# A matmul with bias and residual: 1024-row super tiles, and x transposed as fp32 words of two bf16

## The chip, the cores and the metric

The kernel runs on one core of a Trainium2 chip. The metric is the device time of one launch in microseconds (us), lower is better. "Span" is the time from the first to the last instruction in the one profiled execution; a timed run is 1.7 to 1.9 us longer than its span here. The runs compared below are of the same, fast state, with two exceptions that are marked: two experiments had a single look each, which has no state, and one run of the last version was slow.

PE does the matmuls and transposes (PEld in the profile is the loading of its stationary operand, the one held while the columns of the moving operand stream past it). ACT casts, DVE copies and adds, GpSimd (POOL) adds, and SP issues the transfers. SBUF and PSUM are memories on the chip; the results of PE go to PSUM. The "chain" of a profile is the work that ended last, followed back at each step to what released it.

## The reference

```python
batch, m, k, n = 16, 512, 1024, 768        # all float32
def reference(x, weight, bias, residual):
    return (np.matmul(x, weight) + bias + residual).astype(np.float32)
```

x is 33.6 MB, W 3.1 MB, the residual and the output 25.2 MB each: 87 MB to move, and 64 tiles of 128 rows to multiply.

## The kernel before

A super tile is 512 rows, four consecutive rows on each of 128 partitions, so one row of a transfer is 16 KB (x) or 12 KB (residual, output). ACT casts a tile of x to bf16, PE transposes it in eight 128x128 pieces into one PSUM bank, DVE copies it out as `xt`, and PE multiplies it with W in 16 matmuls, two (512 and 256 columns) for each of eight k chunks. GpSimd adds the bias to the residual in SBUF, and DVE adds the PSUM result onto that. For the first eight tiles the residual is not there yet: DVE puts PSUM plus bias into `tmp`, and GpSimd adds `tmp` to the residual later.

```python
J, HEAD, X_BUFS, RO_BUFS = 4, 3, 3, 7
HEAD_ORDER = [("x", 0), ("w", 0), ("x", 1), ("w", 1), ("w", 2), ("x", 2), ("w", 3), ...]
...
    def transp(t):
        pt = ring(ps, "pt", t, 2, [P, n_k, P], BF16)
        for k in range(n_k):                                   # 8 pieces
            nc.tensor.transpose(out=pt[:, k, :], in_=xb[t][:, ts(k, P)], identity=ident)
        xt[t] = ring(sb, "xt", t, 4, [P, n_k, P], BF16)
        nc.vector.tensor_copy(out=xt[t], in_=pt)
    def mm(t, k, n0, nl):
        nc.tensor.matmul(po[t][:, n0:n0 + nl], lhsT=xt[t][:, k, :], rhs=w_sb[:, k, n0:n0 + nl], ...)
...
    for _ in range(WARM_MM): ...            # 11 matmuls on zeros, to warm the clock
    for kind, i in HEAD_ORDER: ...          # three tiles at once, as x and W arrive
...
    for t in range(HEAD, n_t):
        cast(t + 2)
        if (t + 2) % J == J - 1:
            S = (t + 2) // J
            load_x(S + X_BUFS); load_res(S + 2); store(S - 1)
        transp(t + 1)
        ... 16 matmuls of tile t ...
        finish(t - 1)                       # DVE: PSUM + row (or tmp, for t < 8)
        pool_add(...)                       # GpSimd
    ...
    for n0, nl in chunks:                   # last tile: each chunk has its own store
        ... ; finish(n_t - 1, n0, nl); store(S, J - 1, J, n0, nl)
```

(Here and in the edits below, wrappers such as `K_(...)`, which keeps the program order, are left out in places.)

Of the kernel before, what the change touches and what calls it, by code (L numbers as in the profile page):

```python
# [9 lines left out]
FP32 = mybir.dt.float32  # L10
BF16 = mybir.dt.bfloat16
P = 128
J = 4
HEAD = 3
X_BUFS = 3
RO_BUFS = 7
TMP_BUFS = 4
EARLY = 8
WARM_MM = 11
HEAD_ORDER = [  # L20
    ("x", 0), ("w", 0), ("x", 1), ("w", 1), ("w", 2), ("x", 2),
    ("w", 3), ("w", 4), ("w", 5), ("w", 6), ("w", 7),
]


@with_exitstack
def kernel(
    ctx: ExitStack,
    tc: tile.TileContext,
    x: bass.AP,  # L30
    weight: bass.AP,
    bias: bass.AP,
    residual: bass.AP,
    out: bass.AP,
):
    nc = tc.nc
    x2d = x.flatten_outer_dims()
    res2d = residual.flatten_outer_dims()
    out2d = out.flatten_outer_dims()
    M, K = x2d.shape  # L40
    N = weight.shape[1]
    n_k = K // P
    n_t = M // P
    n_s = n_t // J
    chunks = [(0, 512), (512, N - 512)]

    x_d = x2d.rearrange("(S p j) k -> S p j k", p=P, j=J)
    res_d = res2d.rearrange("(S p j) n -> S p j n", p=P, j=J)
    out_d = out2d.rearrange("(S p j) n -> S p j n", p=P, j=J)
    w_d = weight.rearrange("(ko ki) n -> ki ko n", ki=P)  # L50

    const = ctx.enter_context(tc.tile_pool(name="const", bufs=1))
    sb = ctx.enter_context(tc.tile_pool(name="sb", bufs=1))
    ps = ctx.enter_context(tc.tile_pool(name="ps", bufs=1, space=bass.MemoryType.PSUM))

    def ring(pool, name, i, n, shape, dt):
        return pool.tile(shape, dt, name=name, tag=f"{name}{i % n}", bufs=1)

    def psum_o(i):
        return ring(ps, "psum_o", i, HEAD, [P, N], FP32)  # L60

    x_sb, ro, xb, xt, po, tmp = {}, {}, {}, {}, {}, {}
    K_ = tc.keep_in_program_order

    def load_x(S, j0=0, j1=J):
        if S < n_s:
            if j0 == 0:
                x_sb[S] = ring(sb, "x_tile", S, X_BUFS, [P, J, K], FP32)
            K_(nc.sync.dma_start(out=x_sb[S][:, j0:j1, :], in_=x_d[S, :, j0:j1, :]))

    def load_res(S, j0=0, j1=J):
        if S < n_s:
            if j0 == 0:
                ro[S] = ring(sb, "ro", S, RO_BUFS, [P, J, N], FP32)
            K_(nc.sync.dma_start(out=ro[S][:, j0:j1, :], in_=res_d[S, :, j0:j1, :]))

    def store(S, j0=0, j1=J, n0=0, nl=N):
        if 0 <= S < n_s:
            K_(nc.sync.dma_start(
                out=out_d[S, :, j0:j1, n0:n0 + nl], in_=ro[S][:, j0:j1, n0:n0 + nl]  # L80
            ))

    w_st = [
        ring(sb, "ro", RO_BUFS - 2 + h, RO_BUFS, [P, n_k // 2, N], FP32) for h in range(2)
    ]
    w_sb = const.tile([P, n_k, N], BF16, name="w_sb")


    def cast(t):
        if t < n_t:  # L90
            xb[t] = ring(sb, "xb", t, 4, [P, K], BF16)
            K_(nc.scalar.copy(out=xb[t], in_=x_sb[t // J][:, t % J, :]))  # L92

    def transp(t):
        if t < n_t:
            pt = ring(ps, "pt", t, 2, [P, n_k, P], BF16)
            for k in range(n_k):
                K_(nc.tensor.transpose(out=pt[:, k, :], in_=xb[t][:, ts(k, P)], identity=ident))  # L98
            xt[t] = ring(sb, "xt", t, 4, [P, n_k, P], BF16)
            K_(nc.vector.tensor_copy(out=xt[t], in_=pt))  # L100

    def mm(t, k, n0, nl):
        K_(nc.tensor.matmul(  # L103
            po[t][:, n0:n0 + nl], lhsT=xt[t][:, k, :], rhs=w_sb[:, k, n0:n0 + nl],
            start=(k == 0), stop=(k == n_k - 1),
        ))

    def row(t, n0=0, nl=N):
        return ro[t // J][:, t % J, n0:n0 + nl]

    def pool_add(t):
        if t < n_t:
            r = row(t)
            K_(nc.gpsimd.tensor_add(out=r, in0=r, in1=tmp[t] if t < EARLY else bias_sb))  # L114

    def finish(t, n0=0, nl=N):
        if t < 0:
            return
        p = po[t][:, n0:n0 + nl]
        if t < EARLY:  # L120
            tmp[t] = ring(sb, "tmp", t, TMP_BUFS, [P, N], FP32)
            K_(nc.vector.tensor_add(out=tmp[t], in0=p, in1=bias_sb))  # L122
        else:
            K_(nc.vector.tensor_add(out=row(t, n0, nl), in0=p, in1=row(t, n0, nl)))  # L124


    bias_row = const.tile([1, N], FP32, name="bias_row")
    K_(nc.gpsimd.dma_start(out=bias_row, in_=bias[None, :]))  # L128
    warm = const.tile([P, 512], BF16, name="warm")
    K_(nc.vector.memset(warm, 0.0))  # L130
    ones_row = const.tile([1, P], FP32, name="ones_row")
    K_(nc.vector.memset(ones_row, 1.0))
    warm_a = const.tile([1, 2], FP32, name="warm_a")
    K_(nc.vector.memset(warm_a, 0.0))
    K_(nc.scalar.copy(out=warm_a, in_=warm_a))  # L135
    ident = const.tile([P, P], BF16, name="ident")
    make_identity(nc, ident)

    warm_ps = psum_o(0)
    for _ in range(WARM_MM):  # L140
        K_(nc.tensor.matmul(  # L141
            warm_ps[:, 0:512], lhsT=warm[:, 0:P], rhs=warm, start=True, stop=True
        ))
    bias_ps = psum_o(HEAD - 1)
    for n0, nl in chunks:
        K_(nc.tensor.matmul(  # L146
            bias_ps[:, n0:n0 + nl], lhsT=ones_row, rhs=bias_row[:, n0:n0 + nl],
            start=True, stop=True,
        ))
    bias_sb = const.tile([P, N], FP32, name="bias_sb")  # L150
    K_(nc.vector.tensor_copy(out=bias_sb, in_=bias_ps))  # L151


    seen_x, seen_w = [], []
    for kind, i in HEAD_ORDER:
        if kind == "x":
            load_x(0, i, i + 1)
            cast(i)
            transp(i)
            po[i] = psum_o(i)  # L160
            seen_x.append(i)
        else:
            K_(nc.sync.dma_start(out=w_st[i // 4][:, i % 4, :], in_=w_d[:, i, :]))
            K_(nc.vector.tensor_copy(out=w_sb[:, i, :], in_=w_st[i // 4][:, i % 4, :]))  # L164
            seen_w.append(i)
        for t in seen_x if kind == "w" else [i]:
            for k in [i] if kind == "w" else seen_w:
                for n0, nl in chunks:
                    mm(t, k, n0, nl)
    load_x(0, 3, 4)  # L170
    load_x(1, 0, 2)
    load_res(0, 0, 2)
    load_x(1, 2, 4)
    load_res(0, 2, 4)
    load_x(2)
    load_res(1)
    cast(HEAD)
    transp(HEAD)
    cast(HEAD + 1)
    load_x(3)  # L180
    load_res(2)
    for t in range(HEAD - 1):
        finish(t)
        pool_add(t)


    for t in range(HEAD, n_t):
        cast(t + 2)
        if (t + 2) % J == J - 1:
            S = (t + 2) // J  # L190
            load_x(S + X_BUFS)
            load_res(S + 2)
            store(S - 1)
        transp(t + 1)
        po[t] = psum_o(t)
        if t < n_t - 1:
            for k in range(n_k):
                for n0, nl in chunks:
                    mm(t, k, n0, nl)
        finish(t - 1)  # L200
        if t - 1 < EARLY:
            pool_add(t - 1)
        if t + 1 >= EARLY:
            pool_add(t + 1)
    S = n_s - 1
    store(S, 0, J - 2)
    store(S, J - 2, J - 1)
    for n0, nl in chunks:
        for k in range(n_k):
            mm(n_t - 1, k, n0, nl)  # L210
        finish(n_t - 1, n0, nl)
        store(S, J - 1, J, n0, nl)


# [28 lines left out]
```

## Time and profile before

| | before |
|---|---|
| time, median | 216.97 us (216.23 to 218.88) |
| span | 216.1 us |
| PE busy, share of the chain of waits that ended last | 95%, 93% |
| one tile on PE | 3.05 us: 2.60 for 16 matmuls, 0.45 for 8 transposes |
| rate of the transfers, 30 to 190 us | 427 GB/s |
| rate that one tile in 3.05 us asks for | 430 GB/s |

Read it by the last two rows: PE is the engine that the chain follows, but the transfers run at the same pace. The lines themselves stand in the prediction.

### The profile page before, as it was taken

What the parts mean: (1) busy time and instruction counts of PE and PEld (TensorE: products, weight loads), DVE (VectorE), ACT (ScalarE), POOL (GpSimd) and SP (SyncE); (2) the same over time, 40 slices, a digit from 0 to 9 for tenths busy, and PEclk for the clock granted to TensorE, in tenths of its full rate; (3) what the DMA queues carried; (4) which work ended last, traced back from release to release, by engine and by line L of the source; (5) the groups of instructions that cost most, each with busy time, mean ns of one, the idle gap of its engine ahead of it and who ended that gap; (6) DMA issues with size and microseconds to landing.
All of it is one profiled execution on the core that took longest, in us unless ns stands there. A gap on an engine that the chain in (4) does not pass through costs nothing.

```text
span 216.1 us, 3672 instructions
## 1 busy us (share of the span) xinstructions
PE 205.2 (95%) x1551; PEld 132.4 (61%) x1551; DVE 105.1 (49%) x141; ACT 68.0 (31%) x66; POOL 115.3 (53%) x71
## 2 busy tenths in 40 slices
PE   7678799999999999999999999999999999999992
PEld 2335566666666666666666666666666666666651
DVE  0245365445554455445544555445544555445542
ACT  2314416323332333323332333323332333231000
POOL 2000096669928467390928457290936629099600
PEclk9658999999999999999999999999999999999999
DMA  6999999999999999999999999999999999999654
GB/s 179 393 413 418 441 413 429 428 425 431 428 422 431 425 427 421 434 422 421 440 418 436 426 432 420 431 428 422 434 417 438 421 432 424 434 414 416 260 233 176
DMA packets 9265, 87.28 MB, mean 404 GB/s; under 512 B 1056, under 2 KB 1184, under 8 KB 3360
## 3 DMA queue, kind: packets, MB, share of 16 engines
q1 hardware_dynamic: 9216, 87.04, 96.0%
q8 instruction: 12, 0.20, 0.4%
q14 instruction: 5, 0.04, 0.0%
q0 software_dynamic: 32, 0.00, 0.0%
HBM read 61.87 MB, written 25.17 MB: 403 GB/s over the span
## 4 chain that ended last, share of the span: by engine, by line
PE 93%; DVE 3%; DMA 3%; issue 1%; DVEq 0%; POOLq 0%
PE psum_o L103 78%; PE pt L98 13%; DMA bias_row<-in_bias_dram 3%; PE psum_o L146 1%; DVE xt L100 1%; DVE ro L124 1%; DVE tmp L122 0%; DVE bias_sb L151 0%; DVE w_sb L164 0%; DVEq L124 0%; DVEq L100 0%; POOLq L227 0%; POOLq masks.py:199 0%
## 5 line engine op out<-in xcount | busy, mean ns | idle before, releaser
L103 PE MATMUL psum_o<-w_sb,xt 128*128 128x256 bf16 (+1 forms) x1024 | 178.8, 328 | 4.9 <-DVE xt L100 1.6
L103 PEld LDWEIGHTS <-xt 128*128 128x128 bf16 x1024 | 97.8, 98 | 64.9 <-issue 2.2
L114 POOL TENSOR_TENSOR ro<-ro,bias_sb 128x768 f32<-128x768 f32 x56 | 99.7, 1812 | 59.5 <-DMA ro<-in_residual_dram 59.5
L92 ACT CAST xb<-x_tile 128x1024 bf16<-128x1024 f32 x64 | 66.5, 1046 | 127.0 <-PE pt L98 102.8
L100 DVE COPY xt<-pt 128x1024 bf16<-128x1024 bf16 x64 | 44.3, 692 | 94.6 <-PE pt L98 94.6
L124 DVE TENSOR_TENSOR ro<-psum_o,ro 128x768 f32<-128x768 f32 (+2 forms) x57 | 53.3, 935 | 4.9 <-PE psum_o L103 3.0
L98 PEld LDWEIGHTS <-xb 128*128 128x128 bf16 x512 | 34.9, 100 | 9.1 <-ACT xb L92 0.7
L98 PE MATMUL pt<-ident,xb 128*128 128x128 bf16 x512 | 40.1, 223 | 0.0
L114 POOL TENSOR_TENSOR ro<-ro,tmp 128x768 f32<-128x768 f32 x8 | 14.4, 1811 | 27.7 <-DVE tmp L122 26.3
L122 DVE TENSOR_TENSOR tmp<-psum_o,bias_sb 128x768 f32<-128x768 f32 x8 | 7.5, 948 | 0.0
L141 PE MATMUL psum_o<-warm 128*128 128x512 bf16 x11 | 3.9, 531 | 1.2 <-DVE warm L130 1.2
L151 DVE COPY bias_sb<-psum_o 128x768 f32<-128x768 f32 x1 | 1.0, 958 | 8.0 <-PE psum_o L146 8.0
L164 DVE CAST w_sb<-ro 128x768 bf16<-128x768 f32 x8 | 4.0, 553 | 0.0
L146 PE MATMUL psum_o<-bias_row,ones_row 1*128 1x512 f32 (+1 forms) x4 | 2.3, 720 | 1.7 <-DMA bias_row<-in_bias_dram 1.7
L141 PEld LDWEIGHTS <-warm 128*128 128x128 bf16 x11 | 1.3, 129 | 3.3 <-issue 1.9
L146 PEld LDWEIGHTS psum_o<-bias_row,ones_row 1*128 1x128 f32 x4 | 0.9, 234 | 3.0 <-issue 3.0
L135 ACT ACT_TABLE_LOAD x1 | 1.3, 1283 | 0.7 <-PEq L227 0.7
L128 POOL DMA_DIRECT2D bias_row<-in_bias_dram x1 | 0.6, 646 | 0.8 <-POOLq L227 0.8
L130 DVE MEMSET warm<- 128x256 uint32 x1 | 0.3, 272 | 0.9 <-PEq L227 0.9
masks.py:199 POOL TENSOR_SCALAR_AFFINE_SELECT ident<-ident 128x128 bf16<-128x128 bf16 x1 | 0.3, 292 | 0.1
L227 POOL MEMSET const-float32-0.0<- 128x1 f32 x1 | 0.1, 98 | 0.2 <-issue 0.2
masks.py:197 POOL MEMSET ident<- 128x128 bf16 x1 | 0.2, 224 | 0.0
(6 smaller groups left out, 0.7 us busy)
## 6 DMA issues: line engine op xcount, KB each, us to landing
x_tile<-in_x_dram SPq DMA_DIRECT2D x14, 2048.0 KB, 24.5
ro<-in_residual_dram SPq DMA_DIRECT2D x15, 1536.0 KB, 27.8
out_dram<-ro SPq DMA_DIRECT2D x15, 1536.0 KB, 25.3
ro<-in_weight_dram SPq DMA_DIRECT2D x8, 384.0 KB, 8.5
x_tile<-in_x_dram SPq DMA_DIRECT2D x4, 512.0 KB, 7.2
x_tile<-in_x_dram SPq DMA_DIRECT2D x2, 1024.0 KB, 11.2
ro<-in_residual_dram SPq DMA_DIRECT2D x2, 768.0 KB, 11.7
out_dram<-ro SPq DMA_DIRECT2D x1, 768.0 KB, 3.3
```

The lines of the kernel that those rows point to most:

```text
L92: K_(nc.scalar.copy(out=xb[t], in_=x_sb[t // J][:, t % J, :]))
L98: K_(nc.tensor.transpose(out=pt[:, k, :], in_=xb[t][:, ts(k, P)], identity=ident))
L100: K_(nc.vector.tensor_copy(out=xt[t], in_=pt))
L103: K_(nc.tensor.matmul(po[t][:, n0:n0 + nl], lhsT=xt[t][:, k, :], rhs=w_sb[:, k, n0:n0 + nl], start=(k == 0), stop=(k == n_k - 1),))
L114: K_(nc.gpsimd.tensor_add(out=r, in0=r, in1=tmp[t] if t < EARLY else bias_sb))
L122: K_(nc.vector.tensor_add(out=tmp[t], in0=p, in1=bias_sb))
L124: K_(nc.vector.tensor_add(out=row(t, n0, nl), in0=p, in1=row(t, n0, nl)))
L135: K_(nc.scalar.copy(out=warm_a, in_=warm_a))
L141: K_(nc.tensor.matmul(warm_ps[:, 0:512], lhsT=warm[:, 0:P], rhs=warm, start=True, stop=True))
L146: K_(nc.tensor.matmul(bias_ps[:, n0:n0 + nl], lhsT=ones_row, rhs=bias_row[:, n0:n0 + nl], start=True, stop=True,))
L151: K_(nc.vector.tensor_copy(out=bias_sb, in_=bias_ps))
L164: K_(nc.vector.tensor_copy(out=w_sb[:, i, :], in_=w_st[i // 4][:, i % 4, :]))
```

## The change

The intent: fewer and longer transfers (rows of 32 and 24 KB), and half as many transposes. A pair of neighbouring bf16 values of x is taken as one fp32 word; four fp32 transposes move what eight bf16 ones did. After that the two values of a pair lie beside each other in `xt`, so the stationary operand of a matmul is read with a step of two, and W is loaded so that rows 2p and 2p+1 lie on one partition. The start is different too: W is loaded first, the start on three tiles at once and the warming matmuls are gone, and the last store is one piece.

```diff
-J = 4
+J = 8
+X_SLOTS = 2
+RO_SLOTS = 4
...
-    w_d = weight.rearrange("(ko ki) n -> ki ko n", ki=P)
+    w_d = weight.rearrange("(q p e) n -> p q e n", p=P, e=2)
...
-            for k in range(n_k):
-                K_(nc.tensor.transpose(out=pt[:, k, :], in_=xb[t][:, ts(k, P)], identity=ident))
+            words = XB[t % 3].bitcast(FP32)
+            for q in range(n_q):
+                K_(nc.tensor.transpose(out=pt[:, q, :], in_=words[:, ts(q, P)], identity=ident))
...
-            po[t][:, n0:n0 + nl], lhsT=xt[t][:, k, :], rhs=w_sb[:, k, n0:n0 + nl],
+            PO[t % PS][:, n0:n0 + nl], lhsT=XT[t % 3][:, q, :, e],
+            rhs=w_sb[:, q, e, n0:n0 + nl],
...
+    load_w(0); load_w(1); load_x(0, 0, 2); load_w(2); load_w(3)
+    load_x(0, 2, 4); load_x(0, 4, 8)
+    load_res(0); load_x(1); load_res(1)
...
-        store(S, J - 1, J, n0, nl)
+    store(S, 7, 8)
```

(The last block of loads is written on fewer lines here.)

More of the change, by code (lines that the diff above doesn't have):

```diff
@@ L12 @@
 P = 128
-J = 4
-HEAD = 3
-X_BUFS = 3
-RO_BUFS = 7
-TMP_BUFS = 4
-EARLY = 8
-WARM_MM = 11
-HEAD_ORDER = [
-    ("x", 0), ("w", 0), ("x", 1), ("w", 1), ("w", 2), ("x", 2),
-    ("w", 3), ("w", 4), ("w", 5), ("w", 6), ("w", 7),
-]
+J = 8
+X_SLOTS = 2
+RO_SLOTS = 4
+EARLY = 8
+PS = 3
 @with_exitstack
@@ L41 @@
     N = weight.shape[1]
-    n_k = K // P
+    n_q = K // (2 * P)
     n_t = M // P
@@ L49 @@
     out_d = out2d.rearrange("(S p j) n -> S p j n", p=P, j=J)
-    w_d = weight.rearrange("(ko ki) n -> ki ko n", ki=P)
-    const = ctx.enter_context(tc.tile_pool(name="const", bufs=1))
+    w_d = weight.rearrange("(q p e) n -> p q e n", p=P, e=2)
     sb = ctx.enter_context(tc.tile_pool(name="sb", bufs=1))
     ps = ctx.enter_context(tc.tile_pool(name="ps", bufs=1, space=bass.MemoryType.PSUM))
-    def ring(pool, name, i, n, shape, dt):
-        return pool.tile(shape, dt, name=name, tag=f"{name}{i % n}", bufs=1)
@@ L59, in psum_o, with fixed @@
-    def psum_o(i):
-        return ring(ps, "psum_o", i, HEAD, [P, N], FP32)
-    x_sb, ro, xb, xt, po, tmp = {}, {}, {}, {}, {}, {}
+    def fixed(pool, name, n, shape, dt):
+        return [pool.tile(shape, dt, name=f"{name}", tag=f"{name}{i}", bufs=1) for i in range(n)]
+    X = fixed(sb, "x_tile", X_SLOTS, [P, J, K], FP32)
+    R = fixed(sb, "ro", RO_SLOTS, [P, J, N], FP32)
+    XB = fixed(sb, "xb", 3, [P, K], BF16)
+    XT = fixed(sb, "xt", 3, [P, n_q, P, 2], BF16)
+    PO = fixed(ps, "psum_o", PS, [P, N], FP32)
@@ L63 @@
+    PT = fixed(ps, "pt", 2, [P, n_q, P], FP32)
+    (w_sb,) = fixed(sb, "w_sb", 1, [P, n_q, 2, N], BF16)
+    (bias_sb,) = fixed(sb, "bias_sb", 1, [P, N], FP32)
+    (bias_row,) = fixed(sb, "bias_row", 1, [1, N], FP32)
+    (ones_row,) = fixed(sb, "ones_row", 1, [1, P], FP32)
+    (ident,) = fixed(sb, "ident", 1, [P, P], FP32)
+    (warm_a,) = fixed(sb, "warm_a", 1, [1, 2], FP32)
     K_ = tc.keep_in_program_order
+    w_st, tmp = R[2], R[3]
     def load_x(S, j0=0, j1=J):
         if S < n_s:
-            if j0 == 0:
-                x_sb[S] = ring(sb, "x_tile", S, X_BUFS, [P, J, K], FP32)
@@ L69, in load_x @@
-            K_(nc.sync.dma_start(out=x_sb[S][:, j0:j1, :], in_=x_d[S, :, j0:j1, :]))
+            K_(nc.sync.dma_start(out=X[S % X_SLOTS][:, j0:j1, :], in_=x_d[S, :, j0:j1, :]))
     def load_res(S, j0=0, j1=J):
         if S < n_s:
-            if j0 == 0:
-                ro[S] = ring(sb, "ro", S, RO_BUFS, [P, J, N], FP32)
-            K_(nc.sync.dma_start(out=ro[S][:, j0:j1, :], in_=res_d[S, :, j0:j1, :]))
+            K_(nc.sync.dma_start(out=R[S % RO_SLOTS][:, j0:j1, :], in_=res_d[S, :, j0:j1, :]))
@@ L77, in store, with load_w @@
+    def load_w(q):
+        K_(nc.sync.dma_start(out=w_st[:, 2 * q:2 * q + 2, :], in_=w_d[:, q, :, :]))
+        for e in range(2):
+            K_(nc.vector.tensor_copy(out=w_sb[:, q, e, :], in_=w_st[:, 2 * q + e, :]))
     def store(S, j0=0, j1=J, n0=0, nl=N):
@@ L79, in store, with mm @@
             K_(nc.sync.dma_start(
-                out=out_d[S, :, j0:j1, n0:n0 + nl], in_=ro[S][:, j0:j1, n0:n0 + nl]
-            ))
-    w_st = [
-        ring(sb, "ro", RO_BUFS - 2 + h, RO_BUFS, [P, n_k // 2, N], FP32) for h in range(2)
-    ]
-    w_sb = const.tile([P, n_k, N], BF16, name="w_sb")
+                out=out_d[S, :, j0:j1, n0:n0 + nl],
+                in_=R[S % RO_SLOTS][:, j0:j1, n0:n0 + nl],
+            ))
     def cast(t):
         if t < n_t:
-            xb[t] = ring(sb, "xb", t, 4, [P, K], BF16)
-            K_(nc.scalar.copy(out=xb[t], in_=x_sb[t // J][:, t % J, :]))
+            K_(nc.scalar.copy(out=XB[t % 3], in_=X[t // J % X_SLOTS][:, t % J, :]))
     def transp(t):
         if t < n_t:
-            pt = ring(ps, "pt", t, 2, [P, n_k, P], BF16)
-            for k in range(n_k):
-                K_(nc.tensor.transpose(out=pt[:, k, :], in_=xb[t][:, ts(k, P)], identity=ident))
-            xt[t] = ring(sb, "xt", t, 4, [P, n_k, P], BF16)
-            K_(nc.vector.tensor_copy(out=xt[t], in_=pt))
-    def mm(t, k, n0, nl):
+            words = XB[t % 3].bitcast(FP32)
+            pt = PT[t % 2]
+            for q in range(n_q):
+                K_(nc.tensor.transpose(out=pt[:, q, :], in_=words[:, ts(q, P)], identity=ident))
+            K_(nc.vector.tensor_copy(
+                out=XT[t % 3].rearrange("p q m e -> p (q m e)"),
+                in_=pt.rearrange("p q m -> p (q m)").bitcast(BF16),
+            ))
+    def mm(t, n0, nl, q, e):
         K_(nc.tensor.matmul(
-            po[t][:, n0:n0 + nl], lhsT=xt[t][:, k, :], rhs=w_sb[:, k, n0:n0 + nl],
-            start=(k == 0), stop=(k == n_k - 1),
+            PO[t % PS][:, n0:n0 + nl], lhsT=XT[t % 3][:, q, :, e],
+            rhs=w_sb[:, q, e, n0:n0 + nl],
+            start=(q == 0 and e == 0), stop=(q == n_q - 1 and e == 1),
         ))
     def row(t, n0=0, nl=N):
-        return ro[t // J][:, t % J, n0:n0 + nl]
+        return R[t // J % RO_SLOTS][:, t % J, n0:n0 + nl]
     def pool_add(t):
@@ L113, in pool_add @@
             r = row(t)
-            K_(nc.gpsimd.tensor_add(out=r, in0=r, in1=tmp[t] if t < EARLY else bias_sb))
+            K_(nc.gpsimd.tensor_add(out=r, in0=r, in1=tmp[:, t, :] if t < EARLY else bias_sb))
     def finish(t, n0=0, nl=N):
-        if t < 0:
-            return
-        p = po[t][:, n0:n0 + nl]
+        p = PO[t % PS][:, n0:n0 + nl]
         if t < EARLY:
-            tmp[t] = ring(sb, "tmp", t, TMP_BUFS, [P, N], FP32)
-            K_(nc.vector.tensor_add(out=tmp[t], in0=p, in1=bias_sb))
+            K_(nc.vector.tensor_add(out=tmp[:, t, :], in0=p, in1=bias_sb))
         else:
             K_(nc.vector.tensor_add(out=row(t, n0, nl), in0=p, in1=row(t, n0, nl)))
-    bias_row = const.tile([1, N], FP32, name="bias_row")
-    K_(nc.gpsimd.dma_start(out=bias_row, in_=bias[None, :]))
-    warm = const.tile([P, 512], BF16, name="warm")
-    K_(nc.vector.memset(warm, 0.0))
-    ones_row = const.tile([1, P], FP32, name="ones_row")
     K_(nc.vector.memset(ones_row, 1.0))
-    warm_a = const.tile([1, 2], FP32, name="warm_a")
     K_(nc.vector.memset(warm_a, 0.0))
     K_(nc.scalar.copy(out=warm_a, in_=warm_a))
-    ident = const.tile([P, P], BF16, name="ident")
-    make_identity(nc, ident)
-    warm_ps = psum_o(0)
-    for _ in range(WARM_MM):
-        K_(nc.tensor.matmul(
-            warm_ps[:, 0:512], lhsT=warm[:, 0:P], rhs=warm, start=True, stop=True
-        ))
-    bias_ps = psum_o(HEAD - 1)
+    load_w(0)
+    load_w(1)
+    load_x(0, 0, 2)
+    load_w(2)
+    load_w(3)
+    load_x(0, 2, 4)
+    load_x(0, 4, 8)
+    load_res(0)
+    load_x(1)
+    load_res(1)
+    K_(nc.gpsimd.dma_start(out=bias_row, in_=bias[None, :]))
+    make_identity(nc, ident)
+    bias_ps = PO[PS - 1]
     for n0, nl in chunks:
@@ L149 @@
         ))
-    bias_sb = const.tile([P, N], FP32, name="bias_sb")
     K_(nc.vector.tensor_copy(out=bias_sb, in_=bias_ps))
-    seen_x, seen_w = [], []
-    for kind, i in HEAD_ORDER:
-        if kind == "x":
-            load_x(0, i, i + 1)
-            cast(i)
-            transp(i)
-            po[i] = psum_o(i)
-            seen_x.append(i)
-        else:
-            K_(nc.sync.dma_start(out=w_st[i // 4][:, i % 4, :], in_=w_d[:, i, :]))
-            K_(nc.vector.tensor_copy(out=w_sb[:, i, :], in_=w_st[i // 4][:, i % 4, :]))
-            seen_w.append(i)
-        for t in seen_x if kind == "w" else [i]:
-            for k in [i] if kind == "w" else seen_w:
-                for n0, nl in chunks:
-                    mm(t, k, n0, nl)
-    load_x(0, 3, 4)
-    load_x(1, 0, 2)
-    load_res(0, 0, 2)
-    load_x(1, 2, 4)
-    load_res(0, 2, 4)
-    load_x(2)
-    load_res(1)
-    cast(HEAD)
-    transp(HEAD)
-    cast(HEAD + 1)
-    load_x(3)
-    load_res(2)
-    for t in range(HEAD - 1):
-        finish(t)
-        pool_add(t)
-    for t in range(HEAD, n_t):
+    cast(0)
+    cast(1)
+    transp(0)
+    for t in range(n_t):
         cast(t + 2)
@@ L190 @@
             S = (t + 2) // J
-            load_x(S + X_BUFS)
-            load_res(S + 2)
-            store(S - 1)
+            if S + 2 < n_s - 1:
+                store(S - 1)
+                load_x(S + 2)
+                load_res(S + 2)
+            elif S + 2 == n_s - 1:
+                load_x(S + 2, 0, 4)
+                load_x(S + 2, 4, 8)
+                store(S - 1)
+                load_res(S + 2)
+            else:
+                store(S - 1)
         transp(t + 1)
-        po[t] = psum_o(t)
         if t < n_t - 1:
-            for k in range(n_k):
-                for n0, nl in chunks:
-                    mm(t, k, n0, nl)
-        finish(t - 1)
-        if t - 1 < EARLY:
-            pool_add(t - 1)
+            for q in range(n_q):
+                for e in range(2):
+                    for n0, nl in chunks:
+                        mm(t, n0, nl, q, e)
+        if t > 0:
+            finish(t - 1)
+            if t - 1 < EARLY:
+                pool_add(t - 1)
         if t + 1 >= EARLY:
@@ L205 @@
     S = n_s - 1
-    store(S, 0, J - 2)
-    store(S, J - 2, J - 1)
+    store(S, 0, 4)
+    store(S, 4, 6)
+    store(S, 6, 7)
     for n0, nl in chunks:
-        for k in range(n_k):
-            mm(n_t - 1, k, n0, nl)
+        for q in range(n_q):
+            for e in range(2):
+                mm(n_t - 1, n0, nl, q, e)
         finish(n_t - 1, n0, nl)
-        store(S, J - 1, J, n0, nl)
+    store(S, 7, 8)
 _INS = ['x', 'weight', 'bias', 'residual']
```

## The prediction

> **What bounds the kernel now.** I read the page's first two parts, then the chain, the timeline of two tiles in the middle, the groups, and last the windows of the head and the tail.
>
> ```profile
> PE 205.2 (95%) x1551; PEld 132.4 (61%) x1551; DVE 105.1 (49%) x141; ACT 68.0 (31%) x66; POOL 115.3 (53%) x71
> ...
> PEclk9658999999999999999999999999999999999999
> DMA  6999999999999999999999999999999999999654
> GB/s 179 393 413 418 441 413 429 428 425 431 428 422 431 425 427 421 434 422 421 440 418 436 426 432 420 431 428 422 434 417 438 421 432 424 434 414 416 260 233 176
> ...
> PE 93%; DVE 3%; DMA 3%; issue 1%; DVEq 0%; POOLq 0%
> ```
>
> Two things are full at once. PE carries 93% of the chain, and the DMA row is 9 tenths from the second slice to the thirty-seventh. So PE is followed back as the cause of the end, but the transfers have almost no slack. The timeline shows the PE's step (columns: start, length in us, engine, line, operation):
>
> ```profile
> 99.58 0.61 PE L98 MATMUL pt<-ident,xb 128*128 128x128 bf16 x8
> ...
> 102.62 0.61 PE L98 MATMUL pt<-ident,xb 128*128 128x128 bf16 x8
> ...
> 105.67 0.61 PE L98 MATMUL pt<-ident,xb 128*128 128x128 bf16 x8
> ```
>
> One 128-row tile takes 105.67 - 102.62 = 3.05 us with no gap. The chain in order of time splits it into 2.60 us for 16 matmuls and 0.45 us for 8 transposes (56 ns each). In 3.05 us a tile needs 4 + 3 + 3 KB for each of 128 rows, 1.311 MB, which is 430 GB/s. Between 30 and 190 us the queues moved 427 GB/s on average. The two limits are thus within 1% of each other, and a PE that needs less can gain only what the transfers lose at the two ends. Those are in the windows (stretch: length, busy time of PE, PEld, DVE, ACT, POOL, then clock, DMA share, GB/s):
>
> ```profile
> 0.00:2.00 2.00, 0.81 (x2) 0.28 (x3) 0.41 (x3) 1.26 (x1) 0.96 (x6) 1.00 0.08 18
> 2.00:4.00 2.00, 2.00 (x6) 0.76 (x5) 0.00 (x0) 0.21 (x2) 0.40 (x2) 1.00 0.96 243
> 4.00:6.00 2.00, 1.14 (x5) 0.29 (x3) 0.00 (x0) 0.34 (x1) 0.00 (x0) 1.00 0.92 327
> ...
> 200.00:202.00 2.00, 2.00 (x19) 1.43 (x18) 1.23 (x2) 0.00 (x0) 2.00 (x3) 1.00 0.49 209
> 202.00:204.00 2.00, 2.00 (x20) 1.39 (x18) 0.51 (x2) 0.00 (x0) 1.61 (x1) 1.00 0.56 211
> ...
> 206.00:208.00 2.00, 2.00 (x20) 1.37 (x18) 1.14 (x2) 0.00 (x0) 0.00 (x0) 1.00 0.44 184
> 208.00:210.00 2.00, 2.00 (x14) 1.13 (x12) 0.89 (x2) 0.00 (x0) 0.00 (x0) 1.00 0.42 172
> ```
>
> All 87.28 MB at 427 GB/s are 204.4 us; the span is 216.1. The missing 11.7 us are, by adding up (427 - rate)/427 over two-microsecond windows, some 3.5 us at the head (small first rows, empty queue) and some 8 us after 198 us, where the last stores wait for the PE, one tile at a time. That 8 us, plus what the head can give, is all there is to win.
>
> **What the Trainium skill says.** "DMA: Bandwidth & Descriptors", § Bandwidth, measures 425 GB/s for a 16 MB transfer under a fabric ceiling of 435; this trace's 427 agrees, so I count on no faster rate from longer rows than about 1%. "TensorE: Matmul & The Clock Gate", § Terms, says transpose mode is "4× faster for FP32"; § Back-to-back issue gap gives N/2.4 + 2.5 ns, 56 ns for N = 128, which the 56 ns of the bf16 transposes confirm. No fp32 transpose runs in this trace. What does run is the fp32 bias matmul:
>
> ```profile
> L146 PE MATMUL psum_o<-bias_row,ones_row 1*128 1x512 f32 (+1 forms) x4 | 2.3, 720 | 1.7 <-DMA bias_row<-in_bias_dram 1.7
> L98 PE MATMUL pt<-ident,xb 128*128 128x128 bf16 x512 | 40.1, 223 | 0.0
> L98 PEld LDWEIGHTS <-xb 128*128 128x128 bf16 x512 | 34.9, 100 | 9.1 <-ACT xb L92 0.7
> ```
>
> Two instructions leave four records: two passes each. Some 2.3 us for 768 columns, at a mean clock of about 0.7, are 4 to 5 cycles a column. A quarter of four is one cycle a column, if the skill's factor holds. The same page, § Weight-path perf modes, says that the fast weight load is not used for fp32, and allows a column step up to 1,024 elements; § LDWEIGHTS gives P/1.2, 107 ns for 128 columns. So the stride of two in the new matmul's stationary operand should cost nothing, while an fp32 transpose may be paced by its weight load.
>
> **The change part by part.**
>
> 1. *Transposes.* Removed: 8 x 56 ns = 0.45 us a tile. Added: 4 fp32 ones. At one cycle a column 4 x 56 = 0.22 us; paced by a 107 ns load (or two cycles a column) 4 x 107 = 0.43 us; with four cycles 4 x 216 = 0.86 us. The tile period p becomes 2.82, 3.03 or 3.46 us. The PSUM copy still moves 1024 bf16 from one bank, 692 ns from the group of line 100, off the path. Casts (1.05 us), adds on DVE (0.95) and GpSimd (1.81) are unchanged and all under p.
>
> 2. *Head.* W now lands first, in four 6 KB-row loads, with two of the x tiles between. Before the first output tile the queue carries 3.15 MB of W and 1.05 MB of x: 9.8 us at 427 GB/s from about 2 us. DVE has all 8 W casts (553 ns each), the bias copy (0.96) and then the first x copy (0.69) in its program order, so the first matmul is at about 14.7 us, on a cold clock (about 1.8 us lost), as the 11 warming matmuls are gone. The kernel before runs pieces of tiles 0 to 2 from 11.4 us, but is only done with three tiles at about 26; here three tiles are done by 14.7 + 1.8 + 3p = 25 to 26. No gain on the PE. On the DMA side the rows of 6 to 8 KB in place of 3 to 4 KB should fill the first 10 us better: perhaps 1 us of the 3.5.
>
> 3. *First hand-over.* x of super tile 1 is queued behind W, x 0 and residual 0: 14.7 MB, so it lands at 2.5 + 34.4 = 36.9 us. Its first cast and transpose stand in the PE's order before the matmuls of tile 7. PE reaches them at 14.7 + 1.8 + 7 x 2.82 = 36.2 (p = 2.82) or 37.7 (p = 3.03). A stall of 1 to 3 us: the matmuls of tile 7 start at about 39.0 either way. Before they started at 39.25.
>
> 4. *Middle.* A super tile is 10.49 MB, 24.6 us at 427 GB/s, against 8p = 22.6 us or 24.2 us. Two x slots suffice: slot S is released by the cast of tile 8S+7, when PE begins tile 8S+3, nine tiles ahead of its next use. The store of a super tile needs its last tile, but when the queue is behind, that is about 6 us after x lands, inside the 7.4 us of the residual load that follows. So the queue stays full, and with p = 2.82 the kernel runs at the pace of the transfers.
>
> 5. *Tail.* After the last x there remain one residual and four stores, some 15.7 MB or 37 us; PE needs about 9p = 25 us plus some 3 us for the wait on the last residual. So for p = 2.82 the PE is done before the queue, and the store of the last row (1.7 to 2.3 us to land before) is nearly all that lies bare.
>
> Sum if transfers bound it: about 2.5 us until the queue is at full rate, 204.0 us for the data at 427 GB/s, 1.5 us of tail: 208. Sum if PE bounds it: 39.0 + 56p for the start of the last tile, + 2.6 for it, + about 2.2 for its last addition and store. With p = 3.03 that is 213.5; with 2.95, 209; with 3.46, 237.5.
>
> **The rivals.**
>
> - *The fp32 transposes save nothing* (p about 3.03, paced by weight loads): 212 to 215 us. For it: the skill's remark on fp32 weight loads, and fp32 loads that record 234 ns here, against 100 for bf16. Against it: some of each load should lie under the matmul before.
> - *Four cycles a column, or a weight load that no longer runs ahead* (p = 3.2 to 3.5): 223 to 240 us, the PE stays at the centre of the chain and the DMA row falls. For it: the bias matmul's 4 to 5 cycles. Against it: the skill's sentence on transpose mode.
> - *A dry queue*: longer transfers with only two x slots. If a store waits longer than I worked out, each of the 8 super tiles loses one or two microseconds: 212 to 222 us at any p. Against it: step 4.
> - *Longer rows raise the rate* to 432 GB/s, near the ceiling: 205.5 us.
>
> **Range and chances.** I choose the bound by transfers as most likely, weigh in the PE-bound case at 3.0 us, and put the point at 209. That is 3.6% under 216.73; the limit for "faster" is 212.4. About half of the weight lies at 206 to 210, a quarter at 210 to 215, the rest mostly above. Range 205.5 to 217. Faster 0.68, same 0.20, slower 0.12.
>
> **What would show it.** Right: fp32 transposes of about 56 ns in the chain's pieces (0.22 us for four), gaps on PE ended by the cast waiting for x, the chain shifting to DMA, a DMA row at 9 until the last slice, over 420 GB/s in the last 15 us. Wrong: a tile period at or above 3.05 us without gaps, matmul steps longer than 2.60 us a tile (the strided weights then cost something), a DMA row with holes in the middle, or SP waits on stores that coincide with such holes.

## The result

219.57 us (219.35 to 219.74), against 216.97 for the kernel before: ratio 1.010, 95% interval 1.005 to 1.015, so slower by about 1%. A ratio is the mean time of one kernel's fast runs over that of the other's of the same rounds, so it is not quite the ratio of the medians. The prediction was 209.0 with a range of 205.5 to 217.0; the result lies above it.

The page of the changed kernel, first its busy times, slices and chain:

```profile
PE 199.5 (92%) x1259; PEld 130.3 (60%) x1284; DVE 105.0 (48%) x140; ACT 67.8 (31%) x66; POOL 115.3 (53%) x71
...
DMA  6999999999999999999999999999999999995553
GB/s 245 425 434 451 454 394 425 433 471 418 385 392 430 445 418 433 431 434 419 427 431 447 439 410 428 433 451 413 436 413 421 431 433 433 409 397 236 238 211 131
...
PE 79%; DMA 18%; issue 1%; DVE 1%; ACT 0%; ACTq 0%; DVEq 0%
```

The DMA row was to stay at 9 to the end; it falls to 5, 5, 5 and 3 in the last four slices; before it fell to 6, 5 and 4 in the last three. The transfers do not set the end: PE still does. The timeline says why (two tiles, columns as in the prediction):

```profile
97.88 0.60 PE L96 MATMUL pt<-ident,xb 128*128 128x128 f32 x4
98.31 2.76 PE L103 MATMUL psum_o<-w_sb,xt 128*128 128x512 bf16 x16
...
100.91 0.60 PE L96 MATMUL pt<-ident,xb 128*128 128x128 f32 x4
```

and the chain, which counts each group only up to the start of the next:

```profile
98.04 0.44 PE pt L96 x4
98.48 2.60 PE psum_o L103 x16
```

Four fp32 transposes take from 97.88 to the first matmul at 98.31, and the next tile begins at 100.91: the tile period is 3.03 us here and 3.037 on average from tile 7 to tile 62, 2.60 for the matmuls and 0.44 for the transposes. One fp32 transpose costs 110 ns where a bf16 one cost 56. Half as many at twice the price: the period is 0.01 us shorter than before (3.046 on average), 0.6 us over 55 periods.

The groups have the same two terms (count | busy, mean ns of one | idle before):

```profile
L96 PE MATMUL pt<-ident,xb 128*128 128x128 f32 x256 | 39.2, 278 | 2.7 <-ACT xb L89 2.7
L96 PEld LDWEIGHTS pt<-ident,xb 128*128 128x128 f32 x256 | 30.4, 143 | 11.2 <-issue 2.1
```

256 records for 256 instructions, so one pass each, and 39.2 us busy in all where the 512 bf16 ones had 40.1.

Where the kernel became slower is seen in the chain in order of time (start, length, what; short pieces are left out at the dots):

```profile
0.74 4.43 DMA ro<-in_weight_dram
5.18 33.74 DMA x_tile<-in_x_dram
...
39.02 1.05 ACT xb L89
...
40.12 0.66 PE pt L96 x4
40.78 0.05 issue
40.83 2.55 PE psum_o L103 x15
```

The x of super tile 1 landed at 38.92 us, 33.7 us after its issue, and its first cast began at 39.02. PE had nothing from 38.79 to 40.12. The matmuls of tile 7 start at 40.83, in the kernel before at 39.25. And the end, in the timelines: here

```profile
212.98 1.03 PE L103 MATMUL psum_o<-w_sb,xt 128*128 128x256 bf16 x8 [0.85 <-DVE ro L122]
...
214.05 0.43 DVE L122 TENSOR_TENSOR ro<-psum_o,ro 128x256 f32<-128x256 f32 x1 [1.12 <-PE psum_o L103]
```

and in the kernel before

```profile
213.07 0.42 DVE L124 TENSOR_TENSOR ro<-psum_o,ro 128x256 f32<-128x256 f32 x1 [1.12 <-PE psum_o L103]
```

From the end of the last addition to the end of the span are 218.0 - 214.48 = 3.5 us against 216.1 - 213.49 = 2.6 us. In the windows of the tail (columns as in the prediction)

```profile
200.00:205.00 5.00, 4.95 (x34) 3.40 (x34) 2.04 (x4) 0.00 (x0) 0.53 (x1) 1.00 0.20 82
205.00:210.00 5.00, 4.95 (x33) 3.19 (x33) 2.91 (x4) 0.00 (x0) 0.00 (x0) 1.00 0.58 241
```

PE is busy throughout and the transfers are nearly idle, 82 GB/s for five microseconds: the stores wait for tiles, as before, in larger pieces.

So the difference of the spans, 1.9 us, is put together from +1.6 at tile 7, -0.6 from 55 slightly shorter periods and +0.9 in the tail. (The medians of the timed runs differ by 2.6 us. The other 0.7 us are mostly scatter of the kernel before: the spans of its eleven runs that were timed with the first experiments go from 214.4 to 217.2 us, and the profiled one, 216.1, lies about 0.9 above what its median time corresponds to. What makes one run of it shorter than another is open.)

### The profile page after: what moved, and what is told of

The parts are those of the page before. It is cut to its first block, busy times and chain, and to the rows that moved or that the text cites. A ratio compares the mean times of both kernels' runs of the same rounds, so it can differ in the third digit from the quotient of the medians.

```text
span 218.0 us, 3057 instructions
## 1 busy us (share of the span) xinstructions
PE 199.5 (92%) x1259; PEld 130.3 (60%) x1284; DVE 105.0 (48%) x140; ACT 67.8 (31%) x66; POOL 115.3 (53%) x71
## 4 chain that ended last, share of the span: by engine, by line
PE 79%; DMA 18%; issue 1%; DVE 1%; ACT 0%; ACTq 0%; DVEq 0%
PE psum_o L103 68%; DMA x_tile<-in_x_dram 15%; PE pt L96 11%; DMA ro<-in_weight_dram 2%; DVE ro L122 1%; ACT xb L89 0%; ACTq L89 0%; DVEq L122 0%
## 5 line engine op out<-in xcount | busy, mean ns | idle before, releaser
L103 PE MATMUL psum_o<-w_sb,xt 128*128 128x256 bf16 (+1 forms) x999 | 175.3, 327 | 5.3 <-DVE xt L97 3.1
L103 PEld LDWEIGHTS <-xt 128*128 128x128 bf16 x1024 | 100.7, 98 | 64.7 <-DVE xt L97 3.5
L96 PE MATMUL pt<-ident,xb 128*128 128x128 f32 x256 | 39.2, 278 | 2.7 <-ACT xb L89 2.7
L96 PEld LDWEIGHTS pt<-ident,xb 128*128 128x128 f32 x256 | 30.4, 143 | 11.2 <-issue 2.1
L115 POOL TENSOR_TENSOR ro<-ro 128x768 f32<-128x768 f32 x8 | 14.3, 1810 | 29.3 <-DMA ro<-in_residual_dram 25.7
L142 PE MATMUL psum_o<-bias_row,ones_row 1*128 1x512 f32 (+1 forms) x4 | 2.9, 876 | 6.5 <-DMA bias_row<-in_bias_dram 6.5
L120 DVE TENSOR_TENSOR ro<-psum_o,bias_sb 128x768 f32<-128x768 f32 x8 | 7.6, 947 | 0.0
```

The source lines that it names most:

```text
L96: K_(nc.tensor.transpose(out=pt[:, q, :], in_=words[:, ts(q, P)], identity=ident))
L103: K_(nc.tensor.matmul(PO[t % PS][:, n0:n0 + nl], lhsT=XT[t % 3][:, q, :, e], rhs=w_sb[:, q, e, n0:n0 + nl], start=(q == 0 and e == 0), sto ...
L115: K_(nc.gpsimd.tensor_add(out=r, in0=r, in1=tmp[:, t, :] if t < EARLY else bias_sb))
L120: K_(nc.vector.tensor_add(out=tmp[:, t, :], in0=p, in1=bias_sb))
L142: K_(nc.tensor.matmul(bias_ps[:, n0:n0 + nl], lhsT=ones_row, rhs=bias_row[:, n0:n0 + nl], start=True, stop=True,))
```

## The experiments

My theory after reading the traces: the fp32 transpose's price is the failed step, the rest of the prediction would have held with a cheaper one, and the loss against the kernel before lies at tile 7 and in the last store.

### Eight bf16 transposes in the new kernel

```diff
-            words = XB[t % 3].bitcast(FP32)
-            for q in range(n_q):
-                transpose(out=pt[:, q, :], in_=words[:, ts(q, P)], identity=ident)
+            cols = XB[t % 3].rearrange("m (q p e) -> m q e p", p=P, e=2)
+            for q in range(n_q):
+                for e in range(2):
+                    transpose(out=pt[:, q, e, :], in_=cols[:, q, e, :], identity=ident)
```

(`pt`, `xt` and the identity are bf16, and the stationary operand is `XT[t % 3][:, q, e, :]`, without a step.)

> The changed kernel with eight bf16 transposes a tile in place of four fp32 ones, and nothing else undone. Theory A (an fp32 transpose costs 110 ns, so four cost what eight bf16 ones do): the tile period goes from 3.036 to about 3.046 us, the time rises by some 0.6 us, ratio to the changed kernel's 219.57 within 0.5%: about 220. Rival B (the fp32 transposes carry a hidden cost, for instance a switch between fp32 and bf16 weights or the stride of two in the stationary operand, and are why the new kernel is slower): the time falls to 217 or below.

220.21 us (219.91 to 220.33), correct, 0.6 us above the 219.57 (each was timed in its own session; against the kernel before they are 1.012 and 1.010, with intervals that overlap). The transposes now start 3.04 us apart (94.90 and 97.94 in the timeline). Theory A holds, B falls: fp32 words neither help by more than 0.3% nor hurt, and the step of two in the stationary operand costs nothing, as the 16 matmuls take 2.60 us with and without it.

### One transpose of four

```diff
-            for q in range(n_q):
-                transpose(out=pt[:, q, :], in_=words[:, ts(q, P)], identity=ident)
+            transpose(out=pt[:, 0, :], in_=words[:, ts(0, P)], identity=ident)
```

(The copy takes that quarter only, and `xt` is set to zero once at the start.)

> Wrong result on purpose: the changed kernel with one fp32 transpose and a quarter of the copy per tile. It stands for a kernel whose transposes are cheap; all transfers stay. Theory A (my prediction failed only on the size of the transposes, its pace of the transfers was right): tile period about 2.71 us where PE has data, PE waits for x, the DMA row is 9 tenths to the end, and the time is 208 to 211 us. Rival C (two slots of 1024 rows leave the queue dry, so that the transfers would have bound it at a later time anyway): 214 us or more, with holes in the DMA row.

211.04 us (210.75 to 211.23), relative error 0.87, at the upper edge of theory A. Its output is wrong, which doesn't matter for the time. Its page:

```profile
PE   0529999499999999999999995999959999999981
...
DMA  6999999999999999999999999999999999999994
GB/s 234 420 438 454 432 429 431 411 459 407 442 381 434 415 434 426 437 426 464 400 428 428 447 414 448 395 442 454 428 431 412 418 434 428 443 440 404 435 400 176
...
PE 60%; DMA 35%; ACT 2%; issue 1%; DVE 1%; ACTq 0%; DVEq 0%
```

Now the DMA row stays full to the last slice, the holes are on PE, and the chain has 35% of DMA in it. This is the picture that the prediction had drawn for the changed kernel, 2 us above its number. (The run takes 0.11 us of transposes a tile, less than the predicted 0.22, and also copies less; at 0.22 the period would be 2.82 us, still under the 3.07 us that the transfers of a tile take at 427 GB/s.) The tile period is 2.71 us where PE has data (93.16 to 95.87 and to 98.58 in the timeline). So two slots of 1024 rows do not starve the queue, and rival C falls.

### What sets the 110 ns: 96 columns streamed, or 96 loaded

```diff
-                transpose(out=pt[:, q, :], in_=words[:, ts(q, P)], identity=ident)
+                transpose(out=pt[:, q, 0:96], in_=words[0:96, ts(q, P)], identity=ident[0:96, 0:96])
```

> Wrong result on purpose: each fp32 transpose takes 96 rows of x, so 96 columns stream past a weight load of 128 columns. If the streaming sets the 110 ns[...], a transpose takes 82 ns, four take 0.33 us and the tile period is 2.93 us. If the weight load sets it, it stays at 110 ns and 3.036 us.

and the mirror of it

```diff
-                transpose(out=pt[:, q, :], in_=words[:, ts(q, P)], identity=ident)
+                transpose(out=pt[0:96, q, :], in_=words[:, q * P:q * P + 96], identity=ident)
```

> Wrong result on purpose, the mirror of the run before: the fp32 transposes load 96 columns as weights and stream 128. If the weight load sets the 110 ns, a transpose takes 82 ns and the tile period is 2.93 us. If the streaming sets it, it stays at 110 ns and 3.036 us.

The two that ran (one look each, state unknown, wrong on purpose, relative error 0.50) gave 213.92 and 219.62 us. Two transposes' starts in the timeline of the first

```profile
95.89 0.49 PE L96 MATMUL pt<-ident,xb 96*128 96x96 f32 x4
...
98.82 0.49 PE L96 MATMUL pt<-ident,xb 96*128 96x96 f32 x4
```

and of the second

```profile
94.70 0.60 PE L96 MATMUL pt<-ident,xb 128*96 128x128 f32 x4
...
97.74 0.60 PE L96 MATMUL pt<-ident,xb 128*96 128x128 f32 x4
```

With 96 columns streamed the period is 2.93 us and the chain gives 0.33 us for four transposes, 82 ns each; with 96 columns loaded it stays at 3.04 and 0.44. The stream sets the price, not the weight load. 110 ns for 128 columns and 82 for 96 are 0.86 and 0.85 ns a column, twice the 0.44 of the bf16 transposes (56 ns for 128). If those 0.44 are one cycle, as the prediction reads them, this is two. Two things are not told apart: with a square identity the run with 96 columns also has only 96 rows, and what in the stream takes the second cycle is not shown. The width of the fp32 result alone is not it: the matmuls write fp32 to PSUM too, and their 6144 columns of a tile take 2.60 us, 0.42 ns each.

### The wait at tile 7 and the last store, one by one and together

First the order of two loads:

```diff
-    load_res(0)
     load_x(1)
+    load_res(0)
     load_res(1)
```

> The changed kernel with x of super tile 1 queued ahead of residual 0. Theory: of the 2.6 us by which the changed kernel is behind, 1.6 to 1.8 us are the wait at tile 7 for x of super tile 1, which landed at 39.02 us. Queued one 3.15 MB load earlier it lands at about 31.7, PE does not wait, the matmuls of tile 7 start at 39.1 and not at 40.83, and everything after moves by that: 217.8. Rival: the transfers behind it (residual 0 and 1) come later and the wait only moves to the adds: 219.5.

223.38 us (222.99 to 223.47), correct, 3.8 us slower than the changed kernel. The theory fell, and the rival was too mild. PE does not wait at tile 7 any more (its matmuls start at about 39.6), but the timeline shows where it waits instead:

```profile
38.89 12.45 POOL L115 TENSOR_TENSOR ro<-ro 128x768 f32<-128x768 f32 x7 [36.41 <-DMA ro<-in_residual_dram]
...
51.29 1.81 POOL L115 TENSOR_TENSOR ro<-ro,bias_sb 128x768 f32<-128x768 f32 x1
...
53.14 0.96 DVE L122 TENSOR_TENSOR ro<-psum_o,ro 128x768 f32<-128x768 f32 x1 [6.56 <-POOL ro L115]
...
54.75 4.46 PE L103 MATMUL psum_o<-w_sb,xt 128*128 128x512 bf16 x16 [2.83 <-DVE xt L97]
```

The residual of super tile 0 now lands at 38.9 us. Its seven additions stand in GpSimd's order ahead of the first bias addition of super tile 1, which so ends at 53.1 us. DVE waits 6.6 us for it, the PSUM slot is not freed, and PE stops; its 16 matmuls after that take 4.5 us in place of 2.8, and the page gives that slice a clock of 7 tenths. In the changed kernel GpSimd had begun at 28.14 us. An engine that is busy 53% of the time had a deadline all the same.

Then the last store, in two pieces again:

```diff
         finish(n_t - 1, n0, nl)
-    store(S, 7, 8)
+        store(S, 7, 8, n0, nl)
```

> The changed kernel with its last store in two pieces, each after its own addition, as the kernel before has it. Theory: from the last addition's end to the end of the span there are 3.5 us here against 2.6 in the kernel before, because the last store carries all 768 columns of the last tile: the time falls by about 0.9 us, to 218.7. Rival: the store's time is nearly all fixed latency and the queue is still busy with the store before it: 219.5.

219.05 us (218.79 to 219.24), correct: 0.5 us less, between the two guesses. In the trace the span ends 2.9 us after the last addition, against 3.5 without the edit. (The run and the 219.57 are of different sessions, and their ratios to the kernel before do not differ clearly; the pair that follows is of one session.)

And both edits in one kernel:

```diff
-    load_res(0); load_x(1); load_res(1)
+    load_x(1); load_res(0); load_res(1)
...
-    store(S, 7, 8)
+        store(S, 7, 8, n0, nl)
```

> Both edits of the two runs before together. Theory (head wait and tail are the whole loss, and add up): 219.6 - 1.8 - 0.9 = 216.9, the kernel before within 0.5%. If one of the two hides the other: 217.8 or more.

222.83 us (222.26 to 223.62), correct, 0.55 less than the order of loads alone, in the same session. The store's half microsecond adds up; the head's theory is refuted again, for the reason just shown.

If both deadlines are real, a piece of x must come first, but only a piece:

```diff
+    load_x(1, 0, 4)
     load_res(0)
-    load_x(1)
+    load_x(1, 4, 8)
     load_res(1)
```

> The changed kernel with the split last store, and x of super tile 1 in two halves, the first ahead of residual 0 and the second behind it. Theory (two deadlines in one queue: PE needs the first rows of x of super tile 1 by 38 us, GpSimd needs residual 0 by about 34 us or its chain of seven adds, 1.81 us each, makes the first add of super tile 1 late): x lands at about 27 us, residual 0 at about 34, GpSimd is through with its early adds at 47, residual 1 lands at 47, and neither PE nor DVE waits: the matmuls of tile 7 start at 39.1, the time is 217.3, equal to the kernel before within 0.5%. If residual 0 is still too late by 5 us: 221 or more.

217.57 us (217.20 to 218.38), correct, ratio to the kernel before 1.002 (0.997 to 1.008), 0.3 us from the expected 217.3. In its chain in order of time the matmuls follow one another at the same step through tile 7, which starts at 39.28:

```profile
36.24 2.60 PE psum_o L103 x16
39.28 2.60 PE psum_o L103 x16
42.31 2.60 PE psum_o L103 x16
```

The half moved ahead is worth 219.05 - 217.57 = 1.5 us, the split store 0.5. Together they account for 2.0 of the 2.6 us; the rest is within the interval. The kernel before had both: it splits the last store, and it loads half of x of its (smaller) super tile 1, half of residual 0, and then the other halves. The change had dropped that order of loads, which the cut diff above does not show.

### A version that beats both

First try: the older start on three tiles at once with x and W alternating (`HEAD_ORDER = [("x", 0), ("w", 0), ("x", 1), ("w", 1), ("x", 2), ("w", 2), ("w", 3)]`, 20 warming matmuls), and

```diff
-    load_res(0); load_x(1); load_res(1)
+    load_x(1, 0, 4); load_x(1, 4, 8); load_res(0)
...
-                store(S - 1); load_x(S + 2); load_res(S + 2)
+                load_x(S + 2); load_res(S + 2); store(S - 1)    # residual 1 first, in the first round
```

> A version meant to beat both: the changed kernel's layout, super tiles and fp32 transposes, with the older kernel's interleaved start on three tiles (x and W alternating, 20 warming matmuls), x of super tile 1 in two halves ahead of residual 0, the order x, residual, store in each super tile, and the split last store. Theory: PE (3.036 us a tile) and the transfers (427 GB/s) are both near their limits, so only the ends can give: the matmuls of tile 7 start at 31 to 33 us in place of 40.8, and the end is then set by the transfers, 208 to 210 of span, 209 to 212 timed. Rival: the transfers fall behind in the middle and PE waits for x at every super tile, which gives the head's gain back: 214 or more.

228.21 us (227.45 to 229.24), correct, the slowest of all. The same chain of additions, and worse, as PE was earlier: residual 0 landed at 39.3 us, DVE waited 12.6 us for GpSimd, and the queue ran dry behind it, as x of super tile 4 could not be loaded before the casts of super tile 2 had freed its slot, and those waited for PE (27 us of waiting in SP's own queue, the longest). PE itself waited 9.3 us, before that hole. One slice of its DMA row fell to 3 tenths at 127 GB/s. I had seen neither deadline when I wrote it.

Second try, with the deadlines counted out beforehand:

```diff
+    load_x(0, 4, 6); load_x(0, 6, 8)
+    load_x(1, 0, 4); load_res(0); load_res(1, 0, 4); load_x(1, 4, 8); load_res(1, 4, 8)
...
+                load_x(S + 2); store(S - 1); load_res(S + 2)
...
+        if 9 <= t < 9 + ON_DVE:          # ON_DVE = 4: tiles 4 to 7 are added on DVE
+            u = t - 9 + EARLY - ON_DVE
+            nc.vector.tensor_add(out=row(u), in0=row(u), in1=tmp[:, u, :])
...
+    def slot(t, n0):                     # last tile: second chunk in a free PSUM slot
+        return PO[(t + (t == n_t - 1 and n0 > 0)) % PS]
```

(The bias product stands after the second W load's matmuls, and there are 12 warming matmuls.)

> The start on three tiles again, with what the last runs showed put right: the bias product moved behind the first W matmuls, 12 warming matmuls, x of super tile 0 and 1 in smaller pieces, residual 0 and half of residual 1 ahead of the second half of x of super tile 1, four of the eight early adds on DVE in place of GpSimd, the order x, store, residual in each super tile, and the last tile's second chunk in a free PSUM slot. Theory: no waits after the first three tiles, the matmuls of tile 7 start at 33 to 35 us, the end is 56 x 3.036 us plus about 6.5 later, 209.5 to 211.5 of span and 211 to 213 timed, 2 to 2.6% under the kernel before. Rival (some other deadline at the start is missed by several us): 215 or more.

213.40 us over six runs, one of which (216.20) is slow; the five fast ones go from 212.79 to 214.17 with a median of 212.88, inside the expected 211 to 213. Correct, ratio to the kernel before 0.982 (0.976 to 0.987): 1.8% faster, though whether it is more than 2% stays unclear. Its page:

```profile
PE 202.2 (96%) x1296; PEld 130.6 (62%) x1296; DVE 109.4 (52%) x145; ACT 67.9 (32%) x66; POOL 110.9 (53%) x67
...
DMA  6999999999999999999999999999999999999856
...
PE 95%; DVE 3%; issue 0%
```

The span is 211.0 us, PE is busy for 96% of it, and after 25 us the list of waits has none on PE; the gain is nearly all at the ends. The matmuls of tile 7 start at 35.6 us in the chain (expected 33 to 35), 3.7 us earlier than in the kernel before, and from the start of the last tile to the end are 5.8 us against 6.7; in DVE's order the last four W casts (from 15.67 us) stand behind the bias copy (14.20) and the third tile's copy (15.07), and PE waited for that copy. Of the several edits in it none was tried alone, so how the 4 to 5 us over the run with half of x first divide among them is open.

## Why the prediction was wrong

1. **Transposes.** This step failed: "At one cycle a column 4 x 56 = 0.22 us". The measured term is 0.44 us, twice that: 0.86 ns a column where 0.44 was forecast. The price was mis-sized, and with it the path: the period stayed at 3.037 us where 2.82 was forecast, so PE and not the transfers went on setting the end. The rival "save nothing" had the period right (3.03). The reason I gave for a possible 0.43 ("paced by a 107 ns load") was wrong as well; the other one in the same brackets, two cycles a column, agrees with the two runs with 96 columns. I had the evidence in hand and read it too kindly: the fp32 bias matmul left two records for each instruction, at 4 to 5 cycles in all, so 2 or more for one pass. A transpose is one pass (256 records for 256 instructions), and half of four is two. The skill's "4× faster" carried more weight with me than the count of records.
2. **Bound by transfers.** Right as a mechanism and not reached. With transposes of 0.11 us a tile the run took 211.0 us and the queue was full to the end. The sum of 208 was about 1 us under that run's span of 209.1; also, I compared a sum for the span with timed runs that are 1 to 2 us longer.
3. **Bound by PE.** The formula "39.0 + 56p" gave 213.5 for p = 3.03, with the span at 218.0. The mis-sized terms: tile 7 started at 40.8 and not 39.0; and from the start of the last tile (40.8 + 56 x 3.037 = 210.9 by the formula, 210.4 in the trace, as no transposes stand before the last tile) to the end I allowed 4.8 us where it took 7.6: the last tile's two chunks with an addition between them (0.85 us in which PE waited), then 3.5 us from the last addition to the end where I had "about 2.2" for addition and store. The trace of the kernel before, which I had, shows 6.7 us for the same stretch. So even the right transpose term would have given a number 4.5 us under the span; but it would have said "within 2%", which is what came.
4. **Head.** Right in kind. The first matmuls came at 15.9 us (14.7 predicted), three tiles were done at about 26.5 (25 to 26). The first 16 matmuls took 2.1 us longer than later ones, where I had 1.8 for a cold clock; the clock row shows 9 tenths there, so that the clock is the reason is not shown. The first 10 us of transfers gained 1.1 us, by the same sum over windows (40, 344, 421, 417, 410 GB/s against 18, 243, 327, 389, 415); I had put 1 us.
5. **First hand-over.** The wait was seen beforehand, and its size of 1 to 3 us held (1.3 us of idle PE), in part by luck: PE came to it at 38.8 us, 1.1 later than in the sum, and x was late as well. The landing of x at 36.9 us was 2.0 us early, because I divided bytes by the rate. By the first seven slices of the page the queue had moved 15.4 MB at 38.2 us, more than the 14.7 MB up to the last byte of that x, and still it landed at 38.9. The packed trace has the time at which each of the 16 DMA engines was done with its share of that load: thirteen between 36.9 and 37.2 us, two at 37.6 and 37.7, the last at 38.9. So bytes over rate was right for most of the engines, and one straggler landed 1.2 us after the fifteenth, about the length of the wait of PE; the load before (residual 0) had all sixteen between 27.2 and 28.0. A 16 KB instruction fetch took 1.1 us in the DMA queues at 30.9, about the size of the lag; that it is the cause is not shown. "The matmuls of tile 7 start at about 39.0 either way" was 1.8 us off, and this is most of what made the kernel slower and not equal.
6. **Middle.** Right: no wait of PE in the middle, two slots suffice, long rows did not raise the rate (426 to 433 GB/s in the windows from 80 to 180 us; 427 before).
7. **Tail.** It could not come about while PE was last.

What no step had: the deadline of GpSimd's additions. It did not bind in the changed kernel, but it is why the obvious repair made things worse.

## What to carry to other kernels

Packing two narrow values into one wide word halves the number of PE transposes but not their time: here half as many took the same time, as each streamed column cost twice as much. When an engine and the transfers are within 1% of each other, a rewrite of the middle can win only what the transfers lose at the ends (the run with cheap transposes was 3% under the kernel before), and the ends can be won directly too: there an order of loads is a list of deadlines: write down for each load which engine needs it when, the half-idle one too, and cut a load in pieces where only its first rows are urgent.

## What the Trainium skill lacked or had wrong

- "TensorE: Matmul & The Clock Gate", § Terms, "4× faster for FP32" for transpose mode: it does not say faster than what. Measured: 110 ns for a 128x128 fp32 transpose in a stream, 0.86 ns a column, twice that of a bf16 one (56 ns). The only fp32 matmul here is that of the bias, 1.50 us for 768 columns or 1.95 ns a column in the last version, where the matmuls just before it took 0.46 ns a column: 2.3 times the transpose, not four. No page gives the cycles a column of an fp32 transpose. "SBUF — State Buffer", § A bandwidth-pool intuition that's wrong (but worth ruling out), gives a bf16 moving operand 2 B per lane and cycle; an estimate from it is two cycles for a 4-byte word, which agrees with the 110 and 82 ns, though no run here tells that cause from another.
- The same page, § LDWEIGHTS and § Weight-path perf modes: no fast weight load for fp32, and a column step of up to 1,024 elements allowed with it. The loads of fp32 are longer in the records (143 ns against 99 for bf16) but did not set the pace: with 96 columns loaded in place of 128 it stayed at 110 ns. The page does not say what a step of two costs; here nothing: 2.60 us for 16 matmuls with it and without it.
- The same page, § Part 4: PE-mode transpose, names about 275 ns for a bf16 transpose in a kernel. The records here say 222 ns for bf16 and 278 for fp32, but in a stream they follow each other by 56 and 110 ns. The records overlap, so they are no pace, and the section doesn't give the pace.
- The same page warns of the clock's records (§ Seeing it yourself). This agrees: the page of the changed kernel gives a clock of 9 tenths or more in every slice, while its first 16 matmuls took 4.7 us in place of 2.6.
- "DMA: Bandwidth & Descriptors" has no figure for how far the 16 engines drift apart in a queue of long loads. Here a 4 MB load with 10.5 MB before it was done on thirteen engines by 37.2 us and on the last at 38.9, when over 15.4 MB had already moved in all.
